# Modulation steps a step later, the last tile's sums ahead of its predecessor's closing, and mixer tiles 160 bytes on

## The chip, the cores and the metric

The kernel runs on one core of a Trainium2 chip. Its time is the device time of one execution in microseconds; lower is better. Three runs of the kernel before gave a median of 1155.19 us (1154.14 to 1155.43). All times below are microseconds from the start of the profiled execution's span. The engines are TensorE (PE, with its weight loads as PEld), VectorE (DVE), ScalarE (ACT), GpSimd (POOL) and SyncE (SP). DMAs are issued on the queues of SP and ACT, and each queue issues in order.

## What is computed

One layer on 512 latent tokens and 256 context tokens of width 1024, in float32: a SwiGLU half-step, a mixer of two head groups, and a second SwiGLU half-step. Each is fed by a normalised, modulated input and added back through a normalised, gated output. The modulation rows come from the conditioning vector through a 1024 by 9216 weight.

```
h = adaLN_in(x)                               # rmsnorm(x) * (1 + scale) + shift
z = (silu(h @ w_in_a) * (h @ w_in_b)) @ w_out # first SwiGLU, D_FF = 2816
x = x + 0.5 * gate * rmsnorm(z)
x = x + gate * rmsnorm(mixer(adaLN_in(x)))    # mLSTM heads and pooling heads
x = x + 0.5 * gate * rmsnorm(swiglu(adaLN_in(x)))
```

`scale`, `shift` and `gate` are rows of `w_mod` applied to `silu(c)`; there are nine of them, in blocks 0 to 8 of 1024 columns, and the blocks used for the context tokens have a second stream.

## The kernel before

Every large product is three matmuls: a float32 operand is split into a high part (a cast, on ScalarE, line 82) and a low part (a subtraction, on VectorE, line 79), and TensorE adds high*high, low*high and high*low in PSUM (lines 98 to 100, or 103 where they are kept in the order of the program). So a weight tile of 512 KB costs one DMA, one ScalarE cast and one VectorE subtraction before TensorE can use it.

**First output projection.** It runs over the tokens in two halves of three tiles (`OutPass`, called `first` and `second`). A pass takes the 22 blocks `f` of the hidden width in turn. For each it fetches a slice of the hidden activations that was stored to DRAM (`q<-g`, on ScalarE's DMA queue, line 766), loads a weight block (`raw<-in_ffn_w_out`, on SP's queue, line 771), splits both, and issues 18 matmuls of 128x512. After each block it calls `filler(fill(i))`, which advances the generator `mod_steps` by that many steps. At the end of a pass come the products of its last `tail` blocks and the closing of its tiles.

**Modulation steps.** `mod_steps` works through blocks 2 to 7. One step loads a 512 KB piece of `w_mod` and multiplies it by a column of the conditioning on VectorE (line 696). After eight steps and a pause, a step issues the block's matmuls with ones (line 704), which sum over partitions, then takes the result out of PSUM (ScalarE copy or VectorE line 710) and writes it to DRAM as a row by four small DMAs on ScalarE's queue (line 716). When block 4 is done, `begin_chain` runs: it loads the mixer's small parameters, multiplies `w_q` and `w_k` together (transposes at line 662, copies at 663, the product at 666 and 668), broadcasts the gate row, and turns four modulation rows into columns (`columns`, a DMA, a transpose at line 235 and a copy at 237).

**Second output projection and the end.** `out_g` with `last` set adds the products of the last four blocks into `z` (line 431), squares the sum for the norm (ScalarE, line 149), multiplies by the gate row in place (line 176, which must wait for the square since both use `z`), and, when both halves are there and GpSimd has made the reciprocal root (lines 160 and 144), computes `z*r + x` (line 180) and stores it (line 182). `x` comes from DRAM (line 1389).

**The mixer** keeps its rotating tiles in one pool, `vx` first and `h4` (4 KB each) among those behind it. Its output projection uses `h4` tiles as one operand of 192 matmuls of 128x512.

The order of instructions on each engine is the order in which the program emits them, moved by a scheduler where nothing pins them; `tc.keep_in_program_order` pins one, `tc.issue_after` puts a group behind another instruction.

Of the kernel before, what the change touches and what calls it, by code (L numbers as in the profile page):

```python
# [16 lines left out]
P = 128  # L17
# [27 lines left out]
def tile_layer(ctx: ExitStack, tc: tile.TileContext, x, c, ctxt, c_ctx, w_mod, b_mod, norm_pre, norm_post,  # L45
# [124 lines left out]
    def ada_tile(t, zs, z, halves, xr, gc, store, nxt, junk, half, keep=lambda ins: ins, put=load):  # L170
# [3 lines left out]
        parts = ([slice(0, D)] if zs is None else [slice(h * 512, (h + 1) * 512) for h in range(2)])  # L174
        for h, cs in enumerate(parts):
            mul = V.tensor_mul(z[:, cs], z[:, cs] if zs is None else zs[h], gc[:, cs])
            if nxt is None and t == NTT - 1:
                tc.keep_in_program_order(mul)
        for cs in parts:
            V.scalar_tensor_tensor(out=z[:, cs], in0=z[:, cs], scalar=r, in1=xr[:, cs], op0=ALU.mult, op1=ALU.add)  # L180
            if nxt is None:
                load(store[:, cs], z[:, cs])
        if nxt is None:
            return None
# [55 lines left out]
    class Ffn:  # L240
# [172 lines left out]
        def out_g(self, fs, first, last):  # L413
            ws = [self.out_weights(f, i) for i, f in enumerate(fs)] if fs[0] not in self.wo else [self.wo[f] for f in fs]
            z, backs = self.z, Backs(4)
            junk = self.pool.tile([P, D], BF16, tag="pu", name="junk3", bufs=1) if last else None
            for i, t in enumerate(self.tiles):
                halves = small(2)
                for h in range(2):
# [19 lines left out]
            return backs  # L439

        def run(self, blocks_of, started=()):
# [12 lines left out]
            return self.out_g(groups[-1], False, True)  # L454


    with ExitStack() as sx:
# [213 lines left out]
        def mod_steps(blocks, new, acc, ahead):  # L671
            for blk, streams in blocks:
                accs = {}
# [6 lines left out]
                def gains():  # L680
# [11 lines left out]
                for k in range(KD):  # L692
# [5 lines left out]
                    yield  # L698
# [6 lines left out]
                if ty == 0:  # L705
                    res = new()[:, 0:n]
                    S.copy(res, p)
                else:
                    res = res if ahead else gains()
                    V.scalar_tensor_tensor(out=res, in0=p, in1=res, op1=ALU.mult,  # L710
                                           **(dict(scalar=1.0, op0=ALU.add) if ty == 1 else
                                              dict(scalar=1.0 if j == 1 else 0.5, op0=ALU.mult)))
                for st in streams:
                    rows[(blk, st)] = dpool.tile([1, D], F32, name=f"row{blk}_{st}")
                for st, i, g, cs in at:
# [752 lines left out]
```

## Time and profile before

| | us |
|---|---|
| median of 3 runs (lowest, highest) | 1155.19 (1154.14, 1155.43) |
| profiled execution | 1152.68 |
| its span | 1150.9 |
| TensorE matmuls busy | 1103.6 (96%) |
| VectorE busy | 885.8 (77%) |
| ScalarE busy | 523.1 (45%) |
| GpSimd busy | 104.7 (9%) |

The profiled execution took 1.8 us more than its span and 2.5 us less than the median. TensorE is busy nearly throughout, so the profile is read for the few stretches in which it is not, and for what ended each of those waits. In a timeline the bracket behind an instruction gives how long its engine had been idle and what ended that.

### The profile page before, as it was taken

What the parts mean: (1) busy time and instruction counts of PE and PEld (TensorE: products, weight loads), DVE (VectorE), ACT (ScalarE), POOL (GpSimd) and SP (SyncE); (2) the same over time, 40 slices, a digit from 0 to 9 for tenths busy, and PEclk for the clock granted to TensorE, in tenths of its full rate; (3) what the DMA queues carried; (4) which work ended last, traced back from release to release, by engine and by line L of the source; (5) the groups of instructions that cost most, each with busy time, mean ns of one, the idle gap of its engine ahead of it and who ended that gap; (6) DMA issues with size and microseconds to landing.
All of it is one profiled execution on the core that took longest, in us unless ns stands there. A gap on an engine that the chain in (4) does not pass through costs nothing.

```text
span 1150.9 us, 17187 instructions
## 1 busy us (share of the span) xinstructions
PE 1103.6 (96%) x6610; PEld 1000.7 (87%) x6610; DVE 885.8 (77%) x1309; ACT 523.1 (45%) x904; POOL 104.7 (9%) x139
## 2 busy tenths in 40 slices
PE   4999999999999999999998899999999999999996
PEld 3799999999998787888797787879889999999995
DVE  3798998898994775446629777766899998898865
ACT  4544333333332442335644755558553444444431
POOL 4000000000000000200205054211000000000001
PEclk9999999999999999999999899999999999999998
DMA  9943443543735996247603211135334543433321
GB/s 311 267 137 101 156 136 119 177 137 96 233 113 155 342 359 213 85 168 263 184 12 99 65 65 64 56 128 166 92 111 147 156 141 100 139 110 111 110 74 73
DMA packets 151806, 166.09 MB, mean 144 GB/s; under 512 B 7318, under 2 KB 125590, under 8 KB 151724
## 3 DMA queue, kind: packets, MB, share of 16 engines
q1 hardware_dynamic: 144708, 154.18, 42.2%
q10 hardware_dynamic: 7016, 10.80, 2.7%
q8 instruction: 52, 0.85, 0.3%
q14 instruction: 30, 0.25, 0.1%
HBM read 149.98 MB, written 14.98 MB: 143 GB/s over the span
## 4 chain that ended last, share of the span: by engine, by line
PE 81%; DVE 7%; ACT 3%; DMA 2%; issue 2%; POOL 1%; ACTq 0%; DVEq 0%; POOLq 0%; SPq 0%
PE pa L98 16%; PE pa L99 16%; PE pa L100 16%; PE pa L103 10%; PE pz L103 5%; PE pz L98 4%; PE pz L99 4%; PE pz L100 4%; PE pt L103 3%; DMA raw<-in_ffn_w_out_dram 1%; DVE wins L79 1%; PE pt L106 1%; ACT junk L149 1%; DMA m<-in_w_mod_dram 1%; ACT wins L82 1%
## 5 line engine op out<-in xcount | busy, mean ns | idle before, releaser
L98 PE MATMUL pa<-yh,wins 128*128 128x256 f32 (+1 forms) x768 | 235.6, 307 | 0.9 <-ACT pu L376 0.5
L99 PE MATMUL pa<-yh,wins 128*128 128x256 f32 (+1 forms) x768 | 235.2, 307 | 0.1
L100 PE MATMUL pa<-yl,wins 128*128 128x256 f32 (+1 forms) x768 | 234.9, 306 | 0.0
L79 DVE TENSOR_TENSOR wins<-raw,wins 128x1024 fp32r<-128x1024 f32 (+1 forms) x132 | 141.6, 1074 | 58.4 <-ACT wins L82 30.1
L82 ACT CAST wins<-raw 128x1024 fp32r<-128x1024 f32 (+1 forms) x134 | 123.2, 926 | 96.7 <-PE pa L100 32.0
L98 PEld LDWEIGHTS pa<-yh,wins 128*128 128x128 f32 x768 | 145.7, 190 | 3.8 <-issue 1.3
L99 PEld LDWEIGHTS pa<-yh,wins 128*128 128x128 f32 x768 | 145.8, 190 | 0.9 <-DVE wins L79 0.3
L100 PEld LDWEIGHTS pa<-yl,wins 128*128 128x128 f32 x768 | 145.7, 190 | 0.4
L99 PE MATMUL pa<-th,wins 128*128 128x384 f32 (+1 forms) x388 | 121.4, 313 | 0.5 <-DVE wins L79 0.5
L98 PE MATMUL pa<-th,wins 128*128 128x384 f32 (+1 forms) x388 | 121.4, 314 | 0.5 <-ACT wins L82 0.4
L100 PE MATMUL pa<-tl,wins 128*128 128x384 f32 (+1 forms) x388 | 121.3, 313 | 0.0
L696 DVE SCALAR_TENSOR_TENSOR m<-m,sc,m 128x1024 f32<-128x1024 f32 x72 | 90.1, 1278 | 25.5 <-DMA m<-in_w_mod_dram 21.3
L82 ACT CAST wins<-sw 128x1024 fp32r<-128x1024 f32 x78 | 81.7, 1048 | 59.1 <-PE pa L100 30.6
L79 DVE TENSOR_TENSOR wins<-sw,wins 128x1024 fp32r<-128x1024 f32 x78 | 95.1, 1221 | 10.6 <-PE pa L99 7.9
L103 PE MATMUL pa<-yh,wins 128*128 128x512 f32 (+2 forms) x352 | 96.1, 360 | 0.0
L98 PEld LDWEIGHTS pa<-th,wins 128*128 128x128 f32 x388 | 73.2, 189 | 1.8 <-ACT wins L82 0.9
L99 PEld LDWEIGHTS pa<-th,wins 128*128 128x128 f32 x388 | 73.5, 189 | 0.7 <-DVE wins L79 0.7
L100 PEld LDWEIGHTS pa<-tl,wins 128*128 128x128 f32 x388 | 73.5, 189 | 0.1
L103 PEld LDWEIGHTS pa<-yh,wins 128*128 128x128 f32 x352 | 61.8, 190 | 8.9 <-issue 2.2
L103 PE MATMUL pa<-yl,wins 128*128 128x512 f32 (+2 forms) x176 | 62.1, 353 | 0.5 <-DVE yl L79 0.5
L98 PE MATMUL pz<-wos,gh 128*128 128x512 f32 x144 | 56.6, 393 | 0.8 <-ACT z L429 0.4
L431 DVE TENSOR_TENSOR z<-z,pz 128x512 f32<-128x512 f32 x68 | 46.0, 683 | 13.7 <-PE pz L100 11.6
(409 smaller groups left out, 2208.3 us busy)
## 6 DMA issues: line engine op xcount, KB each, us to landing
raw<-in_ffn_w_in_dram SPq DMA_DIRECT2D x87, 512.0 KB
raw<-in_ffn_w_out_dram SPq DMA_DIRECT2D x56, 512.0 KB
m<-in_w_mod_dram SPq DMA_DIRECT2D x49, 512.0 KB
raw<-in_w_mod_dram SPq DMA_DIRECT2D x19, 512.0 KB
g<-q SPq DMA_DIRECT2D x22, 384.0 KB
q<-g ACTq DMA_DIRECT2D x44, 192.0 KB
raw<-in_w_in_dram SPq DMA_DIRECT2D x16, 512.0 KB
raw<-in_w_out_dram SPq DMA_DIRECT2D x16, 256.0 KB
```

The lines of the kernel that those rows point to most:

```text
L79: return eng.tensor_tensor(out=out_ap, in0=a, in1=b, op=ALU.subtract)
L82: return S.copy(hi, src)
L98: T.matmul(out_ap, lhsT=wh, rhs=xh, start=first, stop=False, **kw)
L99: T.matmul(out_ap, lhsT=wl, rhs=xh, start=False, stop=False, **kw)
L100: T.matmul(out_ap, lhsT=wh, rhs=xl, start=False, stop=last, **kw)
L103: return tc.keep_in_program_order(T.matmul(*args, **kw))
L106: return tc.keep_in_program_order(T.transpose(**kw))
L149: return S.activation(out=junk, in_=src, func=AF.Square, scale=D ** -0.5, accum_out=ssq)
L431: add = V.tensor_add(z[:, i, cols], z[:, i, cols], q)
L696: V.scalar_tensor_tensor(out=accs[st], in0=w, scalar=sc[:, st * KD + k:st * KD + k + 1], in1=accs[st], op0=ALU.mult, op1=ALU.add)
```

## The change

Four things change.

1. In `mod_steps` the taking out of PSUM and the row DMAs go into a closure `end`, which runs with the next block's first step; the matmuls stay where they were, at the end of the block's own steps. There is one step more in all. In the first pass, steps are taken after blocks 5, 7, 9, 11 and 13 to 19 (11 of them) where they were taken after every odd block (10).
2. The turning of rows into columns leaves `begin_chain` for a function `input_columns`, which the first pass calls ahead of its closing.
3. At the end of the second output projection the product with the gate row is written to a tile of the `raw` pool instead of back into `z`, and `done2` returns a closure `close`. For the last tile but one it is held back until the last tile's sums are issued.
4. `vx` takes 12,544 bytes of each partition instead of 12,384, so what lies behind it in the pool moves by 160 bytes. The `h4` tiles then begin at 224 modulo 256 and no longer at 64; `wins`, `q3`, `gh`, `yh` and `raw` begin at 224 both times.

```diff
@@ ada_tile
-        parts = ([slice(0, D)] if zs is None else [slice(h * 512, (h + 1) * 512) for h in range(2)])
+        parts = [slice(h * 512, (h + 1) * 512) for h in range(2)]
...
@@ out_g
+                end = i == len(self.tiles) - 1
+                keep = tc.keep_in_program_order if last and end else lambda ins: ins
+                halves, scaled = small(2), raw() if last else None
...
-                        add = V.tensor_add(z[:, i, cols], z[:, i, cols], q)
-                        if last and i == len(self.tiles) - 1:
-                            tc.keep_in_program_order(add)
+                        keep(V.tensor_add(z[:, i, cols], z[:, i, cols], q))
                     if last:
                         square_to(halves[:, h:h + 1], z[:, i, cols], junk[:, cols])
-                        backs.tick()
+                        if end and h:
+                            held(keep)
+                        keep(V.tensor_mul(scaled[:, cols], z[:, i, cols], self.gains()[:, cols]))
                 if last:
-                    backs.add(self.done(t, z[:, i, :], halves))
+                    close = self.done(t, z[:, i, :], scaled, halves)
+                    if i == len(self.tiles) - 2:
+                        held = close
+                    else:
+                        close(keep)
@@ mod_steps
+            end = None
             for blk, streams in blocks:
+                done = end and end()
...
-                    yield
+                    yield done
+                    done = None
                 yield
...
                     T.matmul(p[g:g + 32], lhsT=ones.broadcast_to([P, 32]), rhs=accs[st][:, cs], start=True, stop=True)
-                if ty == 0:
-                    res = new()[:, 0:n]
-                    S.copy(res, p)
+                def end(blk=blk, streams=streams, j=j, ty=ty, n=n, at=at, p=p, res=res, gains=gains):
+                    if ty == 0:
+                        res = new()[:, 0:n]
+                        S.copy(res, p)
...
+                    for st, i, g, cs in at:
+                        nc.scalar.dma_start(rows[(blk, st)][:, cs], res[g:g + 1])
+                    return blk
+                if ahead:
+                    yield
                 else:
...
+                    yield end()
+            if ahead:
+                yield end()
@@ begin_chain
+        def input_columns():
+            cols = columns("ycol1", [(4, 0), (3, 0), (4, 1), (3, 1)])
+            chain["y"] = [(cols[0], cols[1]), (cols[2], cols[3])]
...
-            cols = columns("ycol1", [(4, 0), (3, 0), (4, 1), (3, 1)])
-            chain["y"] = [(cols[0], cols[1]), (cols[2], cols[3])]
@@ first.run
-        first.run(rows3("th"), lambda i: xr1[:, i], Backs(0), first_backs, lambda i: i % 2, lambda: second.start(4))
+        first.run(rows3("th"), lambda i: xr1[:, i], Backs(0), first_backs,
+                  lambda i: int(i > 3 and (i % 2 == 1 or i > 12)), lambda: (input_columns(), second.start(4)))
@@ mixer
-        vx = pool.tile([P, NTT, NH, P + 1], F32, tag="vx", name="vx")
+        vx = pool.tile([P, 3136], F32, tag="vx", name="vx")[:, 0:NTT * NH * (P + 1)].rearrange(
+            "p (t h e) -> p t h e", t=NTT, h=NH)
...
-                wx = pool.tile([P, 3096], F32R, tag="vx", name="wx")
+                wx = pool.tile([P, 3136], F32R, tag="vx", name="wx")
@@ done2
-        def done2(t, z, halves):
-            xr = raw()
+        def done2(t, z, scaled, halves):
+            r, xr = rstd2(halves), raw()
             load(xr, x2_d[t - 2])
...
+            def close(keep):
+                for cs in (slice(0, 512), slice(512, D)):
+                    keep(V.scalar_tensor_tensor(out=z[:, cs], in0=scaled[:, cs], scalar=r, in1=xr[:, cs],
+                                                op0=ALU.mult, op1=ALU.add))
+                    load(out[(t - 2) * P:(t - 1) * P, cs], z[:, cs])
+            return close
+        f2.gains = lambda: gains2[0]
```

How the instructions stand, at three places. The names are those of the program; a line number of the changed kernel differs from that of the same statement before.

The start of the first output projection, on ScalarE, before. `row` is a modulation row in DRAM, `q<-g` the fetch for the pass's first block, `m<-raw` and `q<-q` the casts for it.

```order
L82 CAST wins<-raw 128x512
L716 DMA row_0_3340<-m_2739 1x512 x2
L716 DMA row_1_3341<-m_2739 1x512 x2
L663 COPY m_3354<-pt 128x512 x2
L668 ACTIVATE wqk<-pt 128x512
L766 DMA q_3406<-g_117 128x384
L82 CAST m_3410<-raw 128x1024
L82 CAST q_3414<-q_3406 128x384
L376 COPY q_3444<-pa 128x384
```

The same place on ScalarE after the change.

```order
L82 CAST wins<-raw 128x512
L781 DMA q_3355<-g_117 128x384
L82 CAST m_3359<-raw 128x1024
L82 CAST q_3363<-q_3355 128x384
L370 COPY q_3393<-pa 128x384
L372 COPY q_3394<-pa 128x384
L722 DMA row_0_3438<-m_2739 1x512 x2
L722 DMA row_1_3439<-m_2739 1x512 x2
L377 ACTIVATE q_3391<-pa 128x384
```

The first block's fetch and casts stand ahead of the row DMAs, and the copies (663) and the product (668) of `w_q` and `w_k` have gone behind the fetches of the next blocks.

A little later in the pass, on VectorE, before. The products with `sc` are modulation steps of line 696; the rows of line 79 are the low parts of the pass's weights (`wins`) and activations (`q3`), two for each block.

```order
L79 TENSOR_TENSOR q3_3622<-q3_3572,q3_3622 128x384
L696 SCALAR_TENSOR_TENSOR m4_3488<-m4_3496,sc_99,m4_3488 128x1024
L696 SCALAR_TENSOR_TENSOR m4_3488<-m4_3541,sc_99,m4_3488 128x1024
L696 SCALAR_TENSOR_TENSOR m4_3488<-m4_3643,sc_99,m4_3488 128x1024
L79 TENSOR_TENSOR wins_3651<-raw_3648,wins_3650 128x1024
L79 TENSOR_TENSOR q3_3654<-q3_3574,q3_3654 128x384
L79 TENSOR_TENSOR wins_3680<-raw_3677,wins_3679 128x1024
```

The corresponding rows after the change, where the modulation steps have line 699.

```order
L79 TENSOR_TENSOR wins_3610<-raw_3607,wins_3609 128x1024
L79 TENSOR_TENSOR q3_3613<-q3_3563,q3_3613 128x384
L79 TENSOR_TENSOR wins_3639<-raw_3636,wins_3638 128x1024
L699 SCALAR_TENSOR_TENSOR m4_3444<-m4_3532,sc_99,m4_3444 128x1024
L79 TENSOR_TENSOR q3_3642<-q3_3565,q3_3642 128x384
L79 TENSOR_TENSOR wins_3668<-raw_3665,wins_3667 128x1024
L79 TENSOR_TENSOR q3_3671<-q3_3567,q3_3671 128x384
L79 TENSOR_TENSOR wins_3697<-raw_3694,wins_3696 128x1024
```

Three modulation products in a row stood between two blocks' low parts; one does now, and a block's pair stands between it and the next.

The end of the second pass, on TensorE, before: 18 products of the last block but four, the matmuls with ones of the last modulation block, and the first products of the closing.

```order
L99 MATMUL pz<-wins,q_4828 128x512
L100 MATMUL pz<-wins,q_4828 128x512
L98 MATMUL pz<-wins,q_4828 128x512
L99 MATMUL pz<-wins,q_4828 128x512
L100 MATMUL pz<-wins,q_4828 128x512
L704 MATMUL pt<-m_4545,ones 32x256 x4
L103 MATMUL pa<-sw,q_4860 128x512 x3
L103 MATMUL pa<-w_4883,q_4886 128x512 x3
```

And after the change.

```order
L98 MATMUL pz<-wins,q_4787 128x512
L99 MATMUL pz<-wins,q_4787 128x512
L100 MATMUL pz<-wins,q_4787 128x512
L708 MATMUL pt<-m_4516,ones 32x256 x4
L98 MATMUL pa<-wins,q_4831 128x512
L99 MATMUL pa<-wins,q_4831 128x512
L100 MATMUL pa<-wins,q_4831 128x512
L98 MATMUL pa<-wins,q_4831 128x512
```

The matmuls with ones stand 18 products of 128x512 earlier.

The end of the program, on VectorE, with the semaphores waited for: from the sums of the last tile but one, before.

```order
L431 TENSOR_TENSOR z<-z,pz 128x512 [waits PE_49]
L176 TENSOR_TENSOR z<-z,gc_9357 128x512 [waits Activation_49]
L431 TENSOR_TENSOR z<-z,pz 128x512 [waits PE_49]
L176 TENSOR_TENSOR z<-z,gc_9357 128x512 [waits Activation_49]
L180 SCALAR_TENSOR_TENSOR z<-z,sm,raw 128x512 [waits DMAHW4_49,Pool_49]
L180 SCALAR_TENSOR_TENSOR z<-z,sm,raw 128x512 [waits DVE_49]
L431 TENSOR_TENSOR z<-z,pa 128x512 [waits PE_49] x2
L176 TENSOR_TENSOR z<-z,gc_9357 128x512 [waits Activation_49] x2
L180 SCALAR_TENSOR_TENSOR z<-z,sm,raw 128x512 [waits DMAHW5_49,DVE_49,Pool_49]
L180 SCALAR_TENSOR_TENSOR z<-z,sm,raw 128x512 [waits DVE_49]
```

And after.

```order
L428 TENSOR_TENSOR z<-z,pz 128x512 [waits PE_49]
L433 TENSOR_TENSOR raw<-z,gc_9357 128x512 [waits DVE_49]
L428 TENSOR_TENSOR z<-z,pz 128x512 [waits PE_49]
L433 TENSOR_TENSOR raw<-z,gc_9357 128x512 [waits DVE_49]
L428 TENSOR_TENSOR z<-z,pa 128x512 [waits PE_49]
L433 TENSOR_TENSOR raw<-z,gc_9357 128x512 [waits DVE_49]
L428 TENSOR_TENSOR z<-z,pa 128x512 [waits PE_49]
L1410 SCALAR_TENSOR_TENSOR z<-raw,sm 128x512 [waits DMAHW0_49,Activation_49,Pool_49]
L1410 SCALAR_TENSOR_TENSOR z<-raw,sm 128x512 [waits Activation_49]
L433 TENSOR_TENSOR raw<-z,gc_9357 128x512 [waits DVE_49]
L1410 SCALAR_TENSOR_TENSOR z<-raw,sm 128x512 [waits DMAHW1_49,Activation_49,Pool_49]
L1410 SCALAR_TENSOR_TENSOR z<-raw,sm 128x512 [waits DVE_49,Activation_49]
```

The products with the gate row no longer wait for ScalarE, and the last tile's two sums and its first product stand ahead of the closing of the tile before. On SP's queue, the loads of `x` for the last three tiles, which stood ahead of all stores, now stand behind the stores of the first tile (one load) and of the second tile (two loads).

## Rows read from the trace of the kernel before

**Rows 1.** The page: busy time of each engine, TensorE's clock in 40 slices.

```profile
PE 1103.6 (96%) x6610; PEld 1000.7 (87%) x6610; DVE 885.8 (77%) x1309; ACT 523.1 (45%) x904; POOL 104.7 (9%) x139
...
PEclk9999999999999999999999899999999999999998
```

**Rows 2.** Busy time by stretch; columns as the first line names them.

```profile
core 0: us, PE busy (x) PEld busy (x) DVE busy (x) ACT busy (x) POOL busy (x), PEclk, DMA share, GB/s
362.00:368.00 6.00, 4.84 (x29) 4.10 (x28) 1.95 (x4) 3.39 (x6) 0.95 (x1) 1.00 0.38 135
390.00:395.00 5.00, 2.18 (x10) 1.48 (x9) 3.73 (x4) 1.56 (x2) 0.00 (x0) 1.00 0.89 331
545.00:550.00 5.00, 2.51 (x16) 1.32 (x8) 2.26 (x4) 2.91 (x5) 0.17 (x1) 1.00 0.01 3
550.00:555.00 5.00, 4.90 (x14) 3.43 (x15) 4.33 (x5) 3.54 (x5) 0.00 (x0) 0.66 0.74 225
```

**Rows 3.** Waits of TensorE, 362 to 368 and 386 to 396; total, times, longest.

```profile
PE pz L98 <- ACT q L82: 1.2, 1, 1.2
...
PE pa L99 <- DVE q L79: 2.8, 1, 2.8
```

**Rows 4.** ScalarE in order of time: start, duration, what [idle before, releaser].

```profile
362.11 0.59 ACT L663 COPY m<-pt 128x512 f32<-128x512 f32 x1 [5.02 <-PE pt L662]
...
363.95 0.38 ACTq L766 DMA_DIRECT2D q<-g  x1
...
366.58 0.51 ACT L82 CAST q<-q 128x384 fp32r<-128x384 f32 x1 [1.11 <-DMA q<-g]
```

**Rows 5.** VectorE in order of time, 391 to 394.

```profile
391.27 1.28 DVE L696 SCALAR_TENSOR_TENSOR m<-m,sc,m 128x1024 f32<-128x1024 f32 x1 [3.75 <-DMA m<-in_w_mod_dram]
...
393.60 0.55 DVE L79 TENSOR_TENSOR q<-q,q 128x384 fp32r<-128x384 f32 x1
```

**Rows 6.** The chain of waits, 374 to 393: start, duration, what.

```profile
374.15 4.14 DMA tlz<-in_ctx_dram
...
378.36 7.78 DMA m<-in_w_mod_dram
...
387.96 4.86 DMA raw<-in_ffn_w_out_dram
```

**Rows 7.** TensorE in order of time, 544 to 556.

```profile
544.70 0.64 PE L704 MATMUL pt<-m,ones 128*32 128x256 f32 x8
...
548.60 0.49 PE L103 MATMUL pa<-w,q 128*128 128x512 f32 x1 [1.67 <-ACT q L82]
549.91 1.07 PE L103 MATMUL pa<-w,q 128*128 128x512 f32 x2 [0.82 <-DVE q L79]
...
555.08 0.84 PE L103 MATMUL pa<-wins,q 128*128 128x512 f32 x3
```

**Rows 8.** ScalarE in order of time, 545 to 548.

```profile
545.86 1.18 ACTq L716 DMA_DIRECT2D row<-m  x4
547.09 1.04 ACT L82 CAST w<-raw 128x1024 fp32r<-128x1024 f32 x1 [8.32 <-DMA row<-m]
```

**Rows 9.** VectorE at the end of the program.

```profile
1141.13 1.41 DVE L180 SCALAR_TENSOR_TENSOR z<-z,sm,raw 128x512 f32<-128x512 f32 x2 [0.84 <-POOL sm L144]
1142.46 1.28 DVE L431 TENSOR_TENSOR z<-z,pa 128x512 f32<-128x512 f32 x2
...
1146.16 1.42 DVE L180 SCALAR_TENSOR_TENSOR z<-z,sm,raw 128x512 f32<-128x512 f32 x2 [0.84 <-POOL sm L144]
```

**Rows 10.** TensorE's last matmul.

```profile
1140.88 0.39 PE L103 MATMUL pa<-wins,gh 128*128 128x512 f32 x1
```

**Rows 11.** SyncE's issues at the end; the duration spans the group.

```profile
1101.08 8.64 SPq L1389 DMA_DIRECT2D raw<-x  x4
1128.79 19.15 SPq L182 DMA_DIRECT2D out_dram<-z  x8
```

**Rows 12.** TensorE in the mixer, the longest group of one form.

```profile
748.39 4.46 PE L103 MATMUL pa<-wins,h 128*128 128x512 f32 x18
```

More of the change, by code (lines that the diff above doesn't have):

```diff
@@ L173, in ada_tile @@
         r = rstd2(halves)
-        parts = ([slice(0, D)] if zs is None else [slice(h * 512, (h + 1) * 512) for h in range(2)])
+        parts = [slice(h * 512, (h + 1) * 512) for h in range(2)]
         for h, cs in enumerate(parts):
-            mul = V.tensor_mul(z[:, cs], z[:, cs] if zs is None else zs[h], gc[:, cs])
-            if nxt is None and t == NTT - 1:
-                tc.keep_in_program_order(mul)
+            V.tensor_mul(z[:, cs], zs[h], gc[:, cs])
         for cs in parts:
             V.scalar_tensor_tensor(out=z[:, cs], in0=z[:, cs], scalar=r, in1=xr[:, cs], op0=ALU.mult, op1=ALU.add)
[L181 to L184, printed above, removed]
         r2 = rstd1(z, junk)
@@ L414, in out_g @@
             ws = [self.out_weights(f, i) for i, f in enumerate(fs)] if fs[0] not in self.wo else [self.wo[f] for f in fs]
-            z, backs = self.z, Backs(4)
+            z, held = self.z, None
             junk = self.pool.tile([P, D], BF16, tag="pu", name="junk3", bufs=1) if last else None
             for i, t in enumerate(self.tiles):
-                halves = small(2)
+                end = i == len(self.tiles) - 1
+                keep = tc.keep_in_program_order if last and end else lambda ins: ins
+                halves, scaled = small(2), raw() if last else None
                 for h in range(2):
@@ L453, in run @@
                     self.in_f(f, blocks_of(f))
-            return self.out_g(groups[-1], False, True)
+            self.out_g(groups[-1], False, True)
     with ExitStack() as sx:
@@ L678, in mod_steps, with gains @@
                 at = [(st, i, 32 * (nq * st + i), slice(i * n, (i + 1) * n)) for st in streams for i in range(nq)]
-                def gains():
+                def gains(j=j, ty=ty, n=n, at=at):
                     gb = new()[:, 0:n]
@@ L704, in mod_steps @@
                     T.matmul(p[g:g + 32], lhsT=ones.broadcast_to([P, 32]), rhs=accs[st][:, cs], start=True, stop=True)
-                if ty == 0:
-                    res = new()[:, 0:n]
-                    S.copy(res, p)
-                else:
[L709 to L715, printed above, removed]
-                    nc.scalar.dma_start(rows[(blk, st)][:, cs], res[g:g + 1])
-                yield blk
+                def end(blk=blk, streams=streams, j=j, ty=ty, n=n, at=at, p=p, res=res, gains=gains):
+                    if ty == 0:
+                        res = new()[:, 0:n]
+                        S.copy(res, p)
+                    else:
+                        res = res if ahead else gains()
+                        V.scalar_tensor_tensor(out=res, in0=p, in1=res, op1=ALU.mult,
+                                               **(dict(scalar=1.0, op0=ALU.add) if ty == 1 else
+                                                  dict(scalar=1.0 if j == 1 else 0.5, op0=ALU.mult)))
+                    for st in streams:
+                        rows[(blk, st)] = dpool.tile([1, D], F32, name=f"row{blk}_{st}")
+                    for st, i, g, cs in at:
[3 more added lines that the diff above has]
+                    yield
+                else:
+                    yield end()
+            if ahead:
+                yield end()
         steps = mod_steps([(b, (0, 1)) for b in (2, 3, 4)] + [(b, (0,)) for b in (5, 6, 7)], m4, m4, True)
@@ L1385, in last_row @@
                         gains2.append(bc_row(row_tile(), (8, 0)))
-        def done2(t, z, halves):
-            xr = raw()
+        def done2(t, z, scaled, halves):
+            r, xr = rstd2(halves), raw()
             load(xr, x2_d[t - 2])
-            return ada_tile(t, [z[:, 0:512], z[:, 512:1024]], z, halves, xr, gains2[0], out[(t - 2) * P:(t - 1) * P, :], None, None, None)
+            def close(keep):
[5 more added lines that the diff above has]
+        f2.gains = lambda: gains2[0]
         f2.scope(pool, done2, lambda: None)
```

1 line of the change is left out of this document (removed).

## The prediction

> **What bounds the kernel now.** TensorE's matmuls are busy for 96% of the span, at a clock that the page shows below full speed in one slice of 40 only [rows 1]. VectorE follows with 77%, ScalarE with 45%. So a faster engine elsewhere buys nothing in general, and what can be won is the idle time of TensorE, its slow stretch, and what runs after its last matmul. I read the page first, then busy time by stretch to find where TensorE is not full, then its waits there, then the timeline of the engine that each wait names, and last the end of the program.
>
> Outside the start and the mixer, whose order the change leaves, three stretches of the output projections are not full [rows 2]. From 362 to 368 TensorE is busy 4.84 of 6.00, so 1.16 are lost. From 390 to 395 it is 2.18 of 5.00, so 2.82. From 545 to 550 it is 2.51 of 5.00, so 2.49, and the next 5 us run at a granted clock of 0.66. That lies between the two levels, 1.2 and 2.4 GHz: two thirds of the stretch at the lower. TensorE had waited 1.67 and 0.82 just before [rows 7]. I price the slow clock at (1 - 0.66) * 5 = 1.7. Behind the last matmul, which ends at 1140.88 + 0.39 = 1141.27 [rows 10], VectorE works until 1146.16 + 1.42 = 1147.58 [rows 9].
>
> **The wait at 366** is for a cast of `q` [rows 3]. The cast stood idle 1.11 for its DMA, which was issued at 363.95, right behind the copies and the product of `w_q` and `w_k` [rows 4]; the copy at 362.11 had kept ScalarE's queue for 5.02. In the changed order the fetch and the casts for the pass's first block come ahead of those copies and of the row DMAs. The fetch needs 366.58 - 363.95 = 2.6; issued even 3 us earlier it has landed before TensorE asks. I take the 1.16 as gone.
>
> **The wait at 390** is for the low part of `q` on VectorE [rows 3], which ran at 393.60 because a modulation product in front of it stood idle until 391.27, for 3.75, on its `w_mod` piece [rows 5]. Three such products stood in a row there. The two loads that ended last took 7.78 and 4.86 [rows 6]. After the change the fills begin at block 5 instead of 1, so one product stands there, with a block's pair of low parts between it and the next, and its load has had two fills' worth of time more. I take the 2.82 as gone. A fill costs VectorE 1.28 [rows 5] per block of 18 matmuls, and the number of fills rises by one, all of it beside TensorE.
>
> **What takes their place in the pass.** The transposes of `w_q` and `w_k` are now between the pass's first products, and TensorE issues in order, so it can stand on the load of `w_k` there. No row shows that. The bounds are 0, if the load is early, and the whole of a load's time, 4.14 [rows 6]. I take 0.5, near the lower end, because TensorE has a dozen products of the pass in front of the transposes while the load is under way. The late part of the pass has a modulation product for every block from 13 on. (A matmul of 128x512 takes 0.225: in [rows 7] two starts in a group of three are (0.84 - 0.39) / 2 apart.) Each block then needs 512 KB of `w_out`, 512 KB of `w_mod` and 192 KB of activations in its 18 * 0.225 = 4.1 us, about 300 GB/s; the stretch 390 to 395 moved 331 [rows 2]. So the pass stays just under the rate that the trace shows, and I price this at 0 and keep it as a rival. The turning of rows into columns goes behind the pass's products: one transpose and one small copy, hidden under the second pass's loads.
>
> **The wait at 546 to 551.** The four row DMAs of the last modulation block hold ScalarE's queue from 545.86 to 547.04, and the cast behind them starts at 547.09 after 8.32 of idleness [rows 8]. They wait for VectorE and that for the matmuls with ones, which TensorE issues at 544.70 only, behind all of the last block's products [rows 7]. ScalarE had room all the time. In the changed order those matmuls stand 18 products earlier, by the same 4.1. Row DMAs, casts and low parts follow them, so the operand that came for TensorE at 548.60 is there at about 544.5, and the one for 549.91 at 545.8. TensorE reaches them at 548.60 - 1.67 = 546.9 and, without that wait, at 549.91 - 0.82 - 1.67 = 547.4. I take all 2.49 as gone, and with the wait the slow clock behind it: 1.7. Together 4.2; the bounds are 0 and 4.2.
>
> **The end.** Before, the last tile's sums start at 1142.46, behind the closing of the tile before (1141.13, 1.41) [rows 9], though TensorE was done at 1141.27. After, the second sum runs at once: 1141.3 to 1142.0. From the end of the sums to the last closing it took 1146.16 - (1142.46 + 1.28) = 2.42: square, GpSimd's root, and back. So the last closing starts at 1144.4 and ends at 1145.8. In those 2.42 VectorE does the closing of the tile before (1.41) and one product with the gate row (0.64, as one of the sums), 2.05 in all, hidden. The gain is 1147.58 - 1145.8 = 1.8. What could spoil it is SP's queue: `x` was loaded from 1101.08 on, well ahead [rows 11], and is now issued behind the stores. The stores of the first tile go out from 1128.79 [rows 11], and the second tile's `x` behind them, at about 1129.5, lands with the 4.86 of [rows 6] at 1134.4. Its closing could run at 1129.4 + 3 * 0.64 + 2.42 = 1133.7, so it is late by 0.7; that delays this closing, not TensorE. The last two are issued behind the second tile's stores, near 1135.9, and land by about 1141; they are needed at 1142.0 and 1144.4. So it holds by a microsecond, and I take 1.8. The other bound is a landing of 7.78 [rows 6]: the second `x` at 1137.3, the last two issued at 1138.8 and landed at 1146.6, then two closings and a product, 3.5, to 1150.1, a loss of 2.5.
>
> **The mixer tiles.** A group of 18 matmuls with an `h4` operand takes (4.46 - 0.39) / 17 = 0.239 a matmul [rows 12], against 0.225 for the same shape with `q3` [rows 7]. There are 192, so at most 192 * 0.014 = 2.7, if all of it is the address. The trace of before has no `h4` tile at another address, and some of the 0.014 will be other waits in the group. I take 1.0 and keep 0 and 2.7. The Trainium skill ("SBUF — State Buffer", the note on cachelines in the section "Door 1: The DMA port swizzle (why `[64,N]` ≈ `[32,N]`)") has lines of 16 bytes and a penalty for crossing from one to the next. A shift of 160 bytes is ten whole lines, so by that rule this part gives nothing, and the sum below would be 9.5; no row here tests it.
>
> **The sum.** 1.16 + 2.82 - 0.5 + 4.2 + 1.8 + 1.0 = 10.5. The profiled execution took 1152.68 (1.8 more than its span, unchanged) and would take 1142.2. It lies 2.5 below the median of the runs, so against the median of 1155.19 the forecast is 1144.7.
>
> **The rivals.**
> - The mixer's address does nothing, the rest as above: 9.5 gained, 1145.7. For it: the `h4` tiles differ from the others in more than their address, so the cause of the 0.239 is open. Chance 0.24. (This is what the Trainium skill's rule on cachelines, above, comes to.)
> - The waits of the first pass move instead of going: VectorE stands on `w_mod` at another block, or TensorE on `w_k`, and 4.0 + 0.5 of it comes back. For it: 7.78 for a load at 378, and a DMA channel at 0.89 [rows 2, 6]. Against it: the fills start later and are spread. 6 gained: 1149. Chance 0.14.
> - `x` lands late at the end: 1.8 turns into the loss of 2.5. 6.2 gained: 1149. For it: three loads queued behind stores. Against it: DMA is nearly idle there. Chance 0.05.
> - ScalarE's row DMAs still come late at 545, because VectorE's product in front of them waits: 4.2 less, 6.3 gained, 1148.9. Chance 0.05.
> - The waits are set by the DMA rate and not by the order, so the change doesn't do what it says: each comes back elsewhere, 1155. Chance 0.05.
> - Slower. The modulation products of blocks 13 to 19, one for each block, find their `w_mod` pieces late, each with VectorE's two low parts behind it. One such wait cost TensorE 2.8 at 390. Four of the seven give 11.2, which outweighs the 10.5; from the fourth on the kernel is slower, and five give 14.0, or 1158.7. Against it: the rate reckoned above. Chance 0.05.
>
> **How the numbers follow.** The forecast, 1144.7, has a chance of 0.42. Its own range with the bounds of its terms is 1142 to 1147. The rivals at 1145.7, 1149, 1149 and 1148.9 carry another 0.48, so 1142 to 1150 holds a little over 8 in 10, part of each rival's spread falling out. A measurement of this kernel tells a change from none from about 0.2% on, 2.3 us. Faster is then 0.42 + 0.24 + 0.14 + 0.05 + 0.05 = 0.90, the same 0.05, slower 0.05.
>
> **What would show it.** TensorE is full from 362 to 440, but for one short wait before a transpose of `w_k`; there is no wait for `q` behind the last modulation block, and the clock there stays at full speed. No VectorE product of line 699 is idle for over 2 us in the late blocks of the first pass. From the last matmul's end to VectorE's last closing it is 4.5 us, where it was 6.3. The group of 18 takes 4.2, where it took 4.46. The prediction is wrong if TensorE's busy share in the first pass stays where it was, or if `raw<-x` is named as what ended a wait of the last two closings.

## The result and the profile after

| | before | after |
|---|---|---|
| median of 4 runs, us | 1154.66 | 1143.09 |
| lowest, highest | 1152.83, 1155.43 | 1142.53, 1143.56 |
| span of the profiled execution | 1150.9 | 1140.7 |

The ratio is 0.9898 (95% interval 0.9885 to 0.9910): 11.6 us less by the medians, 10.2 by the two profiled executions. The forecast was 1144.7, in a range from 1142 to 1150. It held.

The first lines of the page of the changed kernel, to lay beside [rows 1]:

```profile
PE 1099.7 (96%) x6610; PEld 999.2 (88%) x6610; DVE 886.3 (78%) x1309; ACT 523.5 (46%) x904; POOL 104.7 (9%) x139
...
PEclk9999999999999999999999899999999999999999
```

TensorE has 3.9 us less of busy time (1103.6 before) for as many matmuls, and the span is 10.2 shorter: most of the gain is idle time. A slice of 29 us is too coarse for it. The clock digit of 8 in the 23rd slice stands as before. [rows 1] has a second one, in the last slice, which the prediction's "one slice of 40" passed over; it lies behind the last matmul [rows 10], where a slower clock costs nothing. The gain shows in the stretches, with the columns of [rows 2] (length, TensorE busy, weight loads, VectorE, ScalarE, GpSimd, granted clock, DMA share, GB/s):

```profile
362.00:368.00 6.00, 6.00 (x36) 6.00 (x35) 2.66 (x5) 1.02 (x2) 0.00 (x0) 1.00 0.40 138
368.00:385.00 17.00, 16.47 (x85) 13.91 (x84) 8.97 (x11) 8.76 (x13) 0.00 (x0) 1.00 0.85 295
...
390.00:395.00 5.00, 5.00 (x24) 4.14 (x23) 3.49 (x6) 2.43 (x4) 0.00 (x0) 1.00 1.03 399
450.00:460.00 10.00, 9.05 (x39) 6.66 (x38) 8.03 (x11) 5.31 (x11) 0.00 (x0) 1.00 0.87 303
545.00:550.00 5.00, 5.00 (x24) 4.14 (x23) 4.71 (x6) 2.88 (x6) 0.34 (x2) 1.00 0.87 278
550.00:555.00 5.00, 5.00 (x24) 4.14 (x23) 2.37 (x5) 2.53 (x6) 1.32 (x3) 1.00 1.15 317
```

The three poor stretches of [rows 2] are full and the clock of 0.66 is gone. Two smaller losses have come: 17.00 - 16.47 = 0.53 between 368 and 385, and 10.00 - 9.05 = 0.95 between 450 and 460. The waits of TensorE over both output projections say what they are (total, times, longest), where [rows 3] and [rows 7] had 1.2, 2.8, 1.7 and 0.8:

```profile
PE pa L103 <- DVE q L79: 0.9, 2, 0.6
PE pt L662 <- DMA m<-in_w_k_dram: 0.5, 1, 0.5
```

The second row is the load of `w_k`, as foreseen. The first stands at 456.20 and 457.81, on the low parts of the pass's last two blocks, behind the late modulation products, which were priced at nothing.

Landmarks of the two traces give the account. Ahead of the output projections, at 353, they are 0.05 apart. TensorE's first matmul with `vx`, in the mixer, stands at 645.71 before and 638.37 after: 7.34 from the output projections. At the last products ahead of the second half-step's own output projection (858.80 and 851.03) it is 7.77, so 0.43 from the mixer. At the last matmul it is 8.44, at VectorE's last closing 9.91, and at the end of the span 10.2: 1.47 from the closing and 0.3 from the last stores. The 0.67 inside the second half-step belongs to no part of the change; its instructions there are the same, and in the other traces the stretch from the mixer's last matmul with `h4` to the last matmul of all takes between 0.5 less and 1.7 more than the 354.4 of the kernel before.

### The profile page after: what moved, and what is told of

Its sections match the earlier page's. It is cut to its first block, busy times and chain, and to the rows that moved or that the text cites. A ratio compares the mean times of both kernels' runs of the same rounds, so it can differ in the third digit from the quotient of the medians.

```text
span 1140.7 us, 17179 instructions
## 1 busy us (share of the span) xinstructions
PE 1099.7 (96%) x6610; PEld 999.2 (88%) x6610; DVE 886.3 (78%) x1309; ACT 523.5 (46%) x904; POOL 104.7 (9%) x139
## 4 chain that ended last, share of the span: by engine, by line
PE 75%; DVE 7%; DMA 5%; issue 4%; ACT 3%; POOL 2%; DVEq 0%; SPq 0%; POOLq 0%; ACTq 0%
PE pa L98 16%; PE pa L99 16%; PE pa L100 16%; PE pa L103 9%; PE pz L103 5%; PE pz L98 4%; PE pz L99 3%; PE pz L100 3%; DMA m<-in_w_mod_dram 3%; PE pt L103 2%; DVE wins L79 1%; DMA raw<-in_ffn_w_out_dram 1%; PE pt L106 1%; DVE m L699 1%; POOL h L1074 1%
## 5 line engine op out<-in xcount | busy, mean ns | idle before, releaser
L79 DVE TENSOR_TENSOR wins<-sw,wins 128x1024 fp32r<-128x1024 f32 x78 | 95.2, 1222 | 11.6 <-PE pa L99 8.5
L428 DVE TENSOR_TENSOR z<-z,pz 128x512 f32<-128x512 f32 x68 | 46.1, 685 | 14.7 <-PE pz L100 11.6
```

The costliest lines, as they stand in the source:

```text
L79: return eng.tensor_tensor(out=out_ap, in0=a, in1=b, op=ALU.subtract)
L428: keep(V.tensor_add(z[:, i, cols], z[:, i, cols], q))
```

## The experiments

Each ratio is against runs of the kernel before on the same chip. That kernel's runs spread widely (1152.8 to 1160.9 over the sets), those with the change's modulation part little, so the ratios carry intervals of 0.1 to 0.2%.

| run | what it has of the change | median us | ratio (95%) |
|---|---|---|---|
| e1 | the closing alone | 1155.34 | 0.9986 (0.9973 to 1.0000) |
| e2 | the modulation part alone | 1144.61 | 0.9907 (0.9884 to 0.9931) |
| e3 | the 160 bytes alone | 1155.40 | 0.9996 (0.9983 to 1.0009) |
| e4 | evacuation later, old fills and one more | 1146.31 | 0.9919 (0.9899 to 0.9939) |
| e5 | new fills alone | 1152.50 | 0.9968 (0.9956 to 0.9980) |
| e6 | the chain's call a step later, alone | 1157.42 | 1.0006 (0.9997 to 1.0016) |
| e7 | one more fill, alone | 1153.21 | 0.9965 (0.9953 to 0.9977) |
| e9 | all of it, again | 1143.53 | 0.9886 (0.9870 to 0.9902) |
| e10 | all of it, fills spread evenly | 1143.12 | 0.9883 (0.9866 to 0.9900) |

**e1, the closing alone.** The edit is the parts of the diff in `ada_tile`, `out_g` and `done2`.

> The kernel before with part 3 alone (gain product into its own tile, last tile's sums ahead of its predecessor's closing). Theory A, the parts add up: from the last matmul's end to VectorE's last closing 4.8 us instead of 6.3, everything ahead of it as before, time 1.5 us lower, ratio about 0.9987. Rival B, the x loads behind the stores hold the last closings: raw<-x ends a wait there, and the time is the same or up to 2.5 us higher.

Measured 0.9986, on the expected 0.9987, with an interval that ends at 1.0000, so it is the trace that tells. From the last matmul's end (1147.04) to VectorE's last closing it took 4.83, against 6.31 before; in every other trace with the old end it is 6.3, and 4.8 in every one with the new. The load of `x` did come late for one closing, the second tile's. VectorE there and at the end:

```profile
1139.15 1.42 DVE L1393 SCALAR_TENSOR_TENSOR z<-raw,sm 128x512 f32<-128x512 f32 x2 [1.54 <-DMA raw<-x]
...
1150.45 1.42 DVE L1393 SCALAR_TENSOR_TENSOR z<-raw,sm 128x512 f32<-128x512 f32 x2 [0.76 <-POOL sm L144]
```

It waited 1.54 for `raw<-x`, and the last closing did not notice, because TensorE's sums set the pace. Theory A holds; what B names happens, at a place where it costs nothing. (The span of this profile is 4 us longer than that of before, ahead of the closing.)

**e2, the modulation part alone.**

> The kernel before with parts 1 and 2 alone (evacuation a step later, new fills, row transposes later). Theory A: the three waits of TensorE (1.2 at 366, 2.8 at 394, 2.5 at 549) and the clock of 0.66 behind the last are gone, a wait of 0.5 for w_k and some 0.9 near 457 come, and TensorE reaches the mixer 7.3 us earlier; time 7 to 9 us lower, ratio 0.992 to 0.994. Rival B, part of the shift that the changed kernel shows ahead of the mixer comes from the other parts: less than 6 us.

Measured 0.9907: 11.8 us less by the medians, where 7 to 9 were expected. The waits at 366, 394 and 549 are gone and one of 0.8 for `w_k` is there, as theory A has it; the 0.9 near 457 did not come, and the mixer is reached 8.35 ahead of before, not 7.3. This part is nearly all of the gain. The product of the ratios of e1, e2 and e3 is 0.9889, between those of the two sets of the whole change (0.9898 and 0.9886), so the parts add up within the intervals. Why the medians give more than the one profile of the kernel before is told below, with the sum.

**e3, the 160 bytes alone.**

```diff
-        vx = pool.tile([P, NTT, NH, P + 1], F32, tag="vx", name="vx")
+        vx = pool.tile([P, 3136], F32, tag="vx", name="vx")[:, 0:NTT * NH * (P + 1)].rearrange(
+            "p (t h e) -> p t h e", t=NTT, h=NH)
```

> The kernel before with part 4 alone (vx 160 bytes longer). Theory A, the address sets the pace of the matmuls with an h4 operand: median spacing 227 ns instead of 234, and 0.4 to 1.3 us less in the mixer, ratio about 0.999. Rival B, the pace in the changed kernel came from something else: 234 ns, no shift, ratio 1.000. Rival C, it moves TensorE but the mixer's chains take it back: 227 ns and ratio 1.000.

The median distance of two starts is 227 ns, in e1 and e2, which leave the address, 234. From the first to the last of the 192 matmuls it takes 56.77, against 57.22 before: 0.45. So the address sets the pace (A), and two thirds of what 192 * 7 ns = 1.3 would give does not show in that stretch, as C has it; that the mixer's own waits take it is likely, and was not followed up. The time itself, 0.9996, tells nothing apart.

**Other addresses.** Three kernels with `vx` longer by 32, 64 and 128 bytes, one profile each:

```diff
-        vx = pool.tile([P, NTT, NH, P + 1], F32, tag="vx", name="vx")
+        vx = pool.tile([P, 3104], F32, tag="vx", ...)   # 3112, 3128
```

> The kernel before with vx 32 bytes longer instead of 160, so the h4 tiles begin at 96 modulo 256. Theory A, an h4 operand is slow because it begins at a multiple of 64: median spacing 227 ns. Theory B, it must begin at the same place modulo 256 as the other operand (224): 234 ns as before.

> The kernel before with vx 64 bytes longer, h4 at 128 modulo 256. Theories A (multiple of 64) and B (same place modulo 256 as the other operand) both expect 234 ns. Theory C, that any shift of the pool's tiles helps: 227 ns.

> The kernel before with vx 128 bytes longer, h4 at 192 modulo 256. After 234 ns at 64, 232 at 96, 231 to 232 at 128 and 227 at 224. Theory A, the pace gets better evenly towards 224: 229 ns. Theory B, only the place of the other operand is free of the cost: 231 or more.

| start of `h4`, modulo 256 | 64 | 96 | 128 | 192 | 224 |
|---|---|---|---|---|---|
| median distance of two starts, ns | 234 | 232 | 231 to 232 | 234 | 227 |

The starts are those of the program's layout; the traces show the pace. A multiple of 64 is not the cause: 96 is slow as well. Nor does it get evenly better towards 224. Of the addresses tried, only the one at which `wins`, the other operand, begins too runs at 227. Whether that is the rule stays open: `wins` was not moved, and all tiles behind `vx` moved together.

**e4, evacuation later, with the old fills.** This was to tell whether the later fills or the closure took away the wait at 390.

```diff
-        first.run(..., lambda i: i % 2, lambda: second.start(4))
+        first.run(..., lambda i: int(i % 2 == 1 or i == 18), lambda: second.start(4))
```

with `mod_steps` as changed, and `columns` left in `begin_chain`.

> The kernel before with the evacuation a step later, but with the fills of before (odd blocks) and one more behind block 18, and the row transposes where they were. Theory A, as the prediction has it, the later start of the fills took away the 2.8 us wait at 394 and the closure the others: the wait near 390 stays (2 to 3 us), those at 366 and 549 go, time about 5 us lower, ratio 0.9957. Rival B, the closure alone moves the modulation products out of the way: all three waits go, time 7 to 9 us lower, ratio 0.993.

Measured 0.9919, and all three waits are gone: rival B. Two short ones have come, at 370.71 and 375.21:

```profile
PE pt L662 <- DMA m<-in_w_q_dram: 0.8, 1, 0.8
PE pt L662 <- DMA m<-in_w_k_dram: 0.8, 1, 0.8
```

VectorE at the place of [rows 5], and TensorE's use of the low part:

```profile
385.96 1.28 DVE L699 SCALAR_TENSOR_TENSOR m<-m,sc,m 128x1024 f32<-128x1024 f32 x1 [5.55 <-DMA m<-in_w_mod_dram]
387.65 1.28 DVE L699 SCALAR_TENSOR_TENSOR m<-m,sc,m 128x1024 f32<-128x1024 f32 x1 [0.41 <-DMA m<-in_w_mod_dram]
...
389.99 0.55 DVE L79 TENSOR_TENSOR q<-q,q 128x384 fp32r<-128x384 f32 x1
```

```profile
391.16 0.39 PE L99 MATMUL pa<-wins,q 128*128 128x512 f32 x1
```

VectorE waited 5.55 for its `w_mod` piece, more than the 3.75 of before, and two products still stand in a row, where three did. The low part was finished at 389.99 + 0.55 = 390.54, and TensorE used it 0.6 later without waiting. It came there 1.6 later for the two short waits; in e6, which has neither, it stands 1.99 at this place. So the empty stretch near 390 is owed in part to waits ahead of it.

**e5, the new fills alone.**

```diff
-        first.run(..., lambda i: i % 2, lambda: second.start(4))
+        first.run(..., lambda i: int(i > 3 and (i % 2 == 1 or i > 12)), lambda: second.start(4))
```

> The kernel before with the new fills alone (blocks 5, 7, 9, 11, 13 to 19; evacuation and chain in place). Theory A, what counts is how far VectorE's low parts are ahead of TensorE when a modulation product waits for its load: the pass still starts with no lead, so the wait at 366 (1.2) stays, the one near 390 goes, and new ones come near 455 where the late fills meet the second pass's start; of the 2.5 at 549 about half goes, since the extra fill moves matmuls and evacuation up together. Time 2 to 6 us lower, ratio 0.995 to 0.998. Rival B, the fills are the main part of the change: 7 us or more, ratio 0.994 or less.

Measured 0.9968, in A's range. TensorE's waits:

```profile
PE pa L99 <- DVE q L79: 2.6, 1, 2.6
PE pz L98 <- ACT q L82: 1.1, 1, 1.1
PE pa L103 <- DVE q L79: 1.0, 2, 0.6
```

The 1.1 at 366 stayed, and of the 2.5 near 549 1.0 is left. The 2.6 is not the old wait at 394, as TensorE's row says:

```profile
456.81 0.50 PE L99 MATMUL pa<-wins,q 128*128 128x512 f32 x1 [2.61 <-DVE q L79]
```

TensorE is not held up near 390 and waits at the end of the pass.

**e6, the chain's call a step later, alone.**

```diff
-                if next(steps, None) == 4:
+                blk = next(steps, None)
+                if due and due.pop():
                     begin_chain()
+                if blk == 4:
+                    due.append(True)
```

> The kernel before with only the call of begin_chain moved to the step after (evacuations and fills in place). Theory A, the closure's effect on the first pass is that the chain's copies and loads no longer stand in front of the pass's first block: the waits at 366 and 390 go, VectorE's lead at the fifth block is above zero, and the 2.5 at 549 with the clock of 0.66 stays; time about 4 us lower, ratio 0.9965. Rival B, it is the later evacuation: 366 and 390 stay, ratio 1.000.

Theory A falls, for the time and the place near 390; B falls too, for the wait at 366 went. TensorE now waits in two places, 1.99 until 391.17 and 3.63 until 454.66, and the time is the same. The stretches around them:

```profile
390.00:395.00 5.00, 3.83 (x12) 3.09 (x13) 5.00 (x7) 1.56 (x2) 0.00 (x0) 0.77 0.91 302
395.00:400.00 5.00, 5.00 (x22) 4.01 (x21) 5.00 (x8) 1.46 (x2) 0.00 (x0) 0.89 1.03 402
...
455.00:460.00 5.00, 5.00 (x18) 3.98 (x18) 5.00 (x7) 1.03 (x2) 0.00 (x0) 0.75 0.90 289
```

The granted clock falls behind both, which in these stretches is (0.23 + 0.11 + 0.25) * 5 = 2.9 more. VectorE near the second place:

```profile
440.37 1.29 DVE L696 SCALAR_TENSOR_TENSOR m<-m,sc,m 128x1024 f32<-128x1024 f32 x1 [3.58 <-DMA m<-in_w_mod_dram]
445.26 1.28 DVE L696 SCALAR_TENSOR_TENSOR m<-m,sc,m 128x1024 f32<-128x1024 f32 x1 [3.60 <-DMA m<-in_w_mod_dram]
...
450.40 2.61 DVE L696 SCALAR_TENSOR_TENSOR m<-m,sc,m 128x1024 f32<-128x1024 f32 x2 [3.52 <-DMA m<-in_w_mod_dram]
...
454.06 0.55 DVE L79 TENSOR_TENSOR q<-q,q 128x384 fp32r<-128x384 f32 x1
```

And the same place in the kernel before:

```profile
450.62 0.55 DVE L79 TENSOR_TENSOR q<-q,q 128x384 fp32r<-128x384 f32 x1
```

A `w_mod` load is issued only when the product before it has freed its tile, so the products follow each other at 4.9 us (440.37, 445.26): 3.6 for the load, 1.3 for the product. The low parts of the pass's 19th and 20th block stand behind the last link. In the kernel before the first of them was finished at 450.62 + 0.55 = 451.17, and TensorE used it at 451.22, with nothing to spare. In e6 it was finished at 454.61, and TensorE used it at 454.66 after 3.63 of waiting, so it was ready for it at 451.03. So time won at the start of the pass is given back there, as long as this row of loads stands in front. In e4 the extra fill and the later evacuation put it behind those two blocks' low parts (their last one ended at 434.6). The later chain alone (e6) and the extra fill alone (e7) leave the row in front; e4 has both, and the later evacuation too. Which of these moves it in e4 was not run apart.

**e7, one more fill, alone.**

> The kernel before with one more fill behind block 18, so that the last modulation block's matmuls and their evacuation both stand one block earlier. Theory A, what costs at 546 is that TensorE issues those matmuls behind the last block's products: the wait for the cast (1.7) and the clock of 0.66 go, about 1.0 of waiting for low parts stays, 366 and 390 stay; time 3 us lower, ratio 0.9975. Rival B, the matmuls only go early with the closure: the wait and the clock stay, ratio 1.000.

Measured 0.9965. The stretch at the second pass's end:

```profile
551.00:556.00 5.00, 4.14 (x17) 3.09 (x18) 4.72 (x6) 2.73 (x5) 0.00 (x0) 1.00 0.85 281
```

With the 0.1 that is lost in the 5 us before it, 1.0 of waiting is left of 2.5, and the clock stays at 1.00: theory A. The waits at 366 and near 394 are as before (1.2 and 2.7).

**e9 and e10, all of it again, and with the fills spread evenly.**

```diff
-                  lambda i: int(i > 3 and (i % 2 == 1 or i > 12)), ...
+                  lambda i: int(i in (4, 5, 7, 8, 10, 11, 13, 14, 16, 17, 18)), ...
```

> The changed kernel once more, as the yardstick for the next one on the same chip: ratio 0.989 to 0.991, TensorE waits of 0.5 for w_k and about 0.9 near 456.

> The changed kernel with its eleven fills of the first pass spread evenly (after blocks 4, 5, 7, 8, 10, 11, 13, 14, 16, 17, 18) and none after the last block. Theory A, the waits of 0.9 near 456 come from modulation products that each wait for a load which the product before releases (3.5 plus 1.3 us a link), with the second pass's first low parts behind them: with fewer links at the end they go, and the time is 0.5 to 1 us below the changed kernel's, 0.05 to 0.1%. Rival B, an earlier fill brings a wait back near 390, where VectorE's lead is smallest: 1 to 3 us more than the changed kernel.

The waits near 456 are gone in e10. What is left for TensorE there, from 340 to 600, is 0.8 for `w_k` and 0.3 at 598, which the kernel before has as well. But the time is the same: 1143.12 and 1143.53, with intervals that cover each other. In the profiles both reach the mixer 7.9 ahead of before, so the 0.4 that e9 waits near 456 is not seen to matter. This version is not shown to be better.

## Why the prediction was right, step by step

**The wait at 366: right.** The fetch that [rows 4] has at 363.95 is now issued at 352.15, and the copy of line 663 comes behind it:

```profile
352.15 0.35 ACTq L781 DMA_DIRECT2D q<-g  x1
...
370.23 0.59 ACT L663 COPY m<-pt 128x512 f32<-128x512 f32 x1 [2.97 <-DMA q<-g]
```

In e6 the later call of the chain alone takes this wait away.

**The wait at 390: gone, by one of the two reasons given.** The step said that one product stands in front of the low part where three did, and that its load has more time. The first is so, and the low part of `q` follows at once; the second is not, for VectorE waits 5.47 where [rows 5] has 3.75.

```profile
385.68 1.28 DVE L699 SCALAR_TENSOR_TENSOR m<-m,sc,m 128x1024 f32<-128x1024 f32 x1 [5.47 <-DMA m<-in_w_mod_dram]
386.88 0.56 DVE L79 TENSOR_TENSOR q<-q,q 128x384 fp32r<-128x384 f32 x1
```

In the kernel before, the first of the three ran a little earlier than that one, at 384.55. But the load for the third, the first of the two in the row of SP, was issued at 385.86, when the first had freed a tile (384.55 + 1.28 = 385.83), and the third ran at 391.27 [rows 5]:

```profile
384.55 1.28 DVE L696 SCALAR_TENSOR_TENSOR m<-m,sc,m 128x1024 f32<-128x1024 f32 x1 [3.07 <-issue]
```

```profile
385.86 2.01 SPq L694 DMA_DIRECT2D m<-in_w_mod_dram  x2
```

After the change TensorE uses that low part at 389.28:

```profile
389.28 0.39 PE L99 MATMUL pa<-wins,q 128*128 128x512 f32 x1
```

It was finished at 386.88 + 0.56 = 387.44, 1.8 ahead: this is VectorE's lead, the time from a finished operand to its use. Before, it was finished at 393.60 + 0.55 = 394.15 [rows 5], and TensorE stood 2.82 for it [rows 3]. The experiments order themselves by that number of products. With three in front the low part is finished at 394 or later. With two it is 390.5 to 391.1 (e4, e6, and e5, whose row this is); with one 386.7 to 387.4 (after, e2, e9, e10):

```profile
390.08 0.55 DVE L79 TENSOR_TENSOR q<-q,q 128x384 fp32r<-128x384 f32 x1
```

TensorE comes for it at 389.2 in e6 and 389.3 after the change, and at 391.2 and 392.0 in e4 and e5, where waits at the start of the pass have held it up. So two products in front cost nothing in a pass that starts late (e4, e5) and 1.99 in one that starts early (e6); the change has one, and 1.8 to spare. What the step missed is that it is not the product's wait that counts, but how early the work behind it is finished.

**The load of `w_k`: right in size,** 0.53 for 0.5. The 0.5 was chosen between 0 and 4.14, so the closeness is luck; e2, e9 and e10 have 0.8.

**The late blocks: priced at 0, cost 0.9.** The prediction divided bytes by time and found room. But the loads are not limited by the rate there; they go one after the other, each released by the product of the last. The chain of waits of the changed kernel:

```profile
439.20 3.30 DMA m<-in_w_mod_dram
442.60 1.30 DVE m L699
443.91 3.19 DMA m<-in_w_mod_dram
```

3.3 and 1.3 in turn. VectorE stands 25.0 us in nine waits for `w_mod` between 360 and 470, where it was 21.3 in nine before. The prediction wanted none over 2 in the late blocks, and they have three of 3.1 to 3.4; the kernel is faster all the same, because all of it but the 0.9 falls where the low parts of the blocks at hand are already finished. That is the mechanism of the rival called slower, with small stakes in the changed kernel (0.9), and with 3.6 in e6 at this place.

**The wait at 546: right.** The matmuls with ones stand 4.8 ahead of the closing's first product, where they stood 0.6 ahead (544.70 in [rows 7]). After, and then that product and a later one in the kernel before:

```profile
538.36 0.64 PE L708 MATMUL pt<-m,ones 128*32 128x256 f32 x8
...
543.14 0.84 PE L103 MATMUL pa<-sw,q 128*128 128x512 f32 x3
...
546.54 1.52 PE L103 MATMUL pa<-w,q 128*128 128x512 f32 x6
```

```profile
545.27 0.96 PE L103 MATMUL pa<-sw,q 128*128 128x512 f32 x3
...
553.69 1.54 PE L103 MATMUL pa<-w,q 128*128 128x512 f32 x6
```

ScalarE sends the row DMAs 6.3 earlier and casts at 540.71, where [rows 8] has 547.09:

```profile
539.53 1.15 ACTq L722 DMA_DIRECT2D row<-m  x4
540.71 1.05 ACT L82 CAST w<-raw 128x1024 fp32r<-128x1024 f32 x1 [4.20 <-DMA row<-m]
```

No wait is left there and the granted clock is 1.00. TensorE is 545.27 - 543.14 = 2.13 ahead at the first of these products and 553.69 - 546.54 = 7.15 at the other, so this place gives 5.0, for 4.2. e7 shows that the extra fill alone goes most of the way: it leaves 1.0 of the 2.5, and the clock at 1.00.

**The end: right, 1.5 for 1.8.** TensorE's last matmul, and VectorE behind it, for [rows 9, 10]:

```profile
1132.44 0.39 PE L103 MATMUL pa<-wins,gh 128*128 128x512 f32 x1
```

```profile
1132.87 0.69 DVE L428 TENSOR_TENSOR z<-z,pa 128x512 f32<-128x512 f32 x1 [1.30 <-PE pa L103]
1133.47 1.41 DVE L1410 SCALAR_TENSOR_TENSOR z<-raw,sm 128x512 f32<-128x512 f32 x2
1134.80 0.69 DVE L433 TENSOR_TENSOR raw<-z,gc 128x512 f32<-128x512 f32 x1
1136.25 1.42 DVE L1410 SCALAR_TENSOR_TENSOR z<-raw,sm 128x512 f32<-128x512 f32 x2 [0.77 <-POOL sm L144]
```

The last sums run at 1132.87 and the closing of the tile before behind them, as forecast. From the sum's end to the last closing it took 1136.25 - 1133.56 = 2.69, not 2.42, because GpSimd's first step on a single column took 1.10 there. For the tile before it took 0.30:

```profile
1129.03 0.30 POOL L160 TENSOR_SCALAR sm<-sm 128x1 f32<-128x1 f32 x1 [4.49 <-ACT junk L149]
...
1134.47 1.10 POOL L160 TENSOR_SCALAR sm<-sm 128x1 f32<-128x1 f32 x1 [4.49 <-ACT junk L149]
```

VectorE stood idle beside the first. Beside the second it ran the closing and the product, from 1133.47 to 1135.49, which the prediction called hidden; so this work seems to have lengthened the step that it was to hide behind. In the kernel before, the step takes 0.79 beside the product with the gate row alone. No run was made for it.

The loads of `x` behind the stores, for [rows 11], are in time; no wait of the last two closings ends on `raw<-x`:

```profile
1120.96 0.41 SPq L1406 DMA_DIRECT2D raw<-x  x1
...
1126.40 0.95 SPq L1406 DMA_DIRECT2D raw<-x  x2
```

**The mixer: 0.45 for 1.0.** The group of 18, which [rows 12] has at 4.46:

```profile
740.97 4.34 PE L103 MATMUL pa<-wins,h 128*128 128x512 f32 x18
```

That is 0.232 a matmul where it was 0.239. The measurement stands against the rival that the address does nothing and, with it, against what the Trainium skill's note on cachelines ("SBUF — State Buffer", "Door 1: The DMA port swizzle (why `[64,N]` ≈ `[32,N]`)") comes to for a shift of ten whole lines. The size was off twice: half of the 0.014 was not the address, and of the rest, 192 * 0.007 = 1.3, a third shows in the mixer.

The sum came out at 10.2 in the profiles for 10.5. Below the forecast are the output projections as a whole, by 0.3 (7.34 for 1.16 + 2.82 - 0.5 + 4.2 = 7.68), the mixer by 0.6 and the closing by 0.3. Above it are the second half-step by 0.7 and the last stores by 0.3, which were not in the sum. Within the output projections the first three terms and the late blocks gave 2.1 for 3.5, and the place at 546 5.0 for 4.2. So the steps are right in kind, and the closeness of the total is in part luck.

The medians differ by 1.1 more than the sum, and the profiled execution of before was one of its fastest. Five other traces, of e1, e3 and the three other addresses, have the same output projections. In each the granted clock is lower there for longer: (1 - clock) * length from 340 to 620 is 3.4 in four of them and 5.1 in the fifth, where it is 1.7 in the profiled execution of before, and 0 after the change. So it is likely that the change usually takes away 1.7 us more than this pair of profiles shows.

## What to carry to other kernels

Before pricing a wait on an engine that feeds the bottleneck, measure its lead at that place: the time from a finished operand to its first use. Count what stands in its queue between the wait and that operand. A wait that uses up less than the lead costs nothing, and one that ends just in time becomes the next bound as soon as work ahead of it is sped up (e6). And a load that waits for its predecessor's consumer to free a buffer has a latency per link and not a rate.

## What was not expected of the hardware

Matmuls of 128x512 with an `h4` operand, the 128x128 one that is loaded as weights, ran at a median of 227, 231 to 232 or 234 ns apart by the address at which that operand begins, with only the pool's tiles moved. The same GpSimd instruction on one column took 0.30 us beside an idle VectorE, 0.79 beside one product with the gate row, and 1.10 beside the closing and a product. After waits of TensorE of about the same length the granted clock was not always the same. In the kernel before, 2.82 at 394 was followed by 1.00, as 2.6 near 457 was in e5, and 2.6 near 396 in e1; but 2.5 at 549 was followed by 5 us at 0.66, and so was, in e7, the wait of 2.7 that ended at 396.55, and waits of 2.6 to 2.8 near 395 in e3 and two of the other addresses:

```profile
395.00:400.00 5.00, 3.45 (x8) 2.76 (x9) 5.00 (x6) 0.51 (x1) 0.00 (x0) 0.66 0.88 294
```

No run was made for what tells these apart. In e1 the 2.5 near 551 were followed by 3.4 us lost to the clock. So the price of waiting 2 to 3 us lies here between its length and 3.4 more.
